# Seven products instead of eight for gate and up in FFN1's first half, with the sampled tokens moved into that half

## The chip, the cores and the metric

The kernel runs on one core of one Trainium2 chip. The metric is device time in microseconds (us) of one launch. A profiled execution gives, beside its time, a trace of every instruction: the engines are TensorE (PE; its weight loads are listed as PEld), VectorE (DVE), ScalarE (ACT), GpSimd (POOL), and SyncE (SP), which here issues nearly all DMAs.

## The reference

One inference step of one decoder layer in float32: 1024 prompt tokens in one sequence, and 32 sampled tokens (8 sequences of 4, with caches). Model width 1024, FFN width 2816.

```python
def swiglu_ffn(x, w_gate, w_up, w_down):
    return (jax.nn.silu(x @ w_gate) * (x @ w_up)) @ w_down

def decoder_layer(x, ...):
    x = x + 0.5 * swiglu_ffn(rms_norm(x, ffn1[0]), ffn1[1], ffn1[2], ffn1[3])
    y, ... = token_mixer(rms_norm(x, mix[0]), ...)
    x = x + y
    x = x + 0.5 * swiglu_ffn(rms_norm(x, ffn2[0]), ffn2[1], ffn2[2], ffn2[3])
```

`token_mixer` projects to 1792 columns, runs an RG-LRU (a causal convolution of 4, two gates, a linear recurrence) beside sliding-window attention (8 query heads on 2 key heads, window 128), normalises both, and projects back. The sampled tokens go through the same layer with their own states and caches.

## The kernel before

**Arithmetic.** Activations lie transposed: 128 rows of the feature dimension on the partitions, tokens in the columns, eight such tiles (KD = 8) for width 1024. Every float32 operand of a product is split into a rounded part `hi` and the remainder `lo`, and a product is three matmuls, hi·hi, hi·lo, lo·hi, into the same PSUM bank. Weights are split on the core: ACT writes `whi` (L423), DVE `wlo` (L425); activations likewise into `xh` and `xl`, the FFN's hidden values into `ha`.

**Halves and units.** Tokens are handled in two halves: half 0 (g = 0) is prompt tokens 0 to 511, half 1 is prompt tokens 512 to 1023 and the 32 sampled tokens, 544 columns (`TW`). A product for half 0 is one matmul of 512 columns (L445 to L447); for half 1 it is two of 272 (CB) in two neighbouring banks (L455, L456). Weights come in units of 128 x 1024 (512 KB): a gate or up unit gives one tile f of 128 of the 22 hidden tiles (NF), with 8 k steps; a down unit gives two output tiles from a group of four hidden tiles (the first group: four outputs from two). A tile is thus a gate and an up unit, `gu(f)`; down units follow some tiles later (`DOWN`).

**Stages.** FFN1 of half 0; FFN1 of half 1 with half 0's mixer merged into it; FFN2 of half 0 with half 1's mixer merged in; FFN2 of half 1. `merge` sets each mixer unit at a position counted in FFN units (`POS`: for half 0 the q units at 5, 5, 27, 28, the out units from 47 on). The first tile of FFN1's half 1 is put before the last four down units of half 0.

**Seven products.** In FFN2's half 1, from its fourth tile on (`plain=3`), `gu7` computes gate and up of a tile together. The pair is seen as a 2 x 2 block matrix (gate and up as rows, the two halves of the 1024 inputs as columns), the tokens as 2 x 2 blocks (two halves of inputs, two times 272 tokens), and a variant of Strassen's scheme needs seven block products, P1 to P7, each 4 k x 3 matmuls of 272 columns (L778), where the plain way needs eight. For that, `sums` forms four sums of weight blocks on DVE (L388), `split_pair` splits seven blocks (L401 on ACT, L403 on DVE) into one of six weight slots each, and the token factors (`x1a`, `T1`, `T2`, `x2b`, `T3`, `x2a`, `T4`) are computed once for the half by `prenorm_pairs`. A pair's raw blocks and sums lie in slots of the pool `big`, eight for a pair. `ev7` joins the products and applies silu.

**Order.** `Sched` sets the order of all instructions when the program is built. Each piece of work is a generator that asks for an engine with an estimated duration and the times of what it depends on; the earliest start goes first, then the smaller priority number. `main` (priority 5) puts TensorE's units in the order of `plan`. `MAINCAP` limits the PSUM banks (of eight) that the units hold to six. On the chip each engine then runs its own list in order and waits on semaphores.

**First half's normalisation.** In FFN1's half 0 (`mode == "late"`) the products start on x times the gain, and the reciprocal root mean square (`rslot`, from `rstd_of`) is multiplied in when the gate product is evicted (`evg`, L644) and again after silu. For other halves `prenorm` normalises before the products (L560 to L569). `evd` (L680) adds a down product to x. `mixed` (L1480 to L1490) normalises the mixer's results into `xh` and `xl` for the out units; L1299 writes attention's output.

Of the kernel before, what the change touches and what calls it, by code (L numbers as in the profile page):

```python
# [75 lines left out]
MODES = (None, "tanh", "tanh")  # L76
MAINCAP = 6
# [144 lines left out]
def layer(ctx: ExitStack, tc, t):  # L222
# [12 lines left out]
    xh = [const.tile([128, KD, TW[g]], F32R, name=f"xh{g}") for g in range(2)]  # L235
    xl = [const.tile([128, KD, TW[g]], F32R, name=f"xl{g}") for g in range(2)]
# [61 lines left out]
    def dP(g, passes=1):  # L298
        return TW[g] / 2400 * passes * 1.01 + 0.01
# [61 lines left out]
    pairs = set()  # L361
    sum_of = {}

    def loader():
        n = 2 * FIRST - 1
        while n + 1 < len(order):
            n += 1
            if n in pairs:
                tk = yield Req("Q", 1.0, tok["xt",], big.soon(8), when=big.has(8), lat=4.0)
                raw_of[n], sum_of[n] = ([big.get()[0] for _ in range(4)] for _ in range(2))  # L370
                for i, r in enumerate(raw_of[n]):
                    SP.dma_start(F(r, 0), t["w"][order[n + i // 2], :, i % 2 * 512:i % 2 * 512 + 512])
                done(("raw", n, 0), tk)
                sc.spawn(sums(n), 2)
                n += 1
                continue
            tk = yield Req("Q", 0.6, raws.soon(), when=raws.has(), lat=4.0)
            raw_of[n] = raws.get()[0]
            load_piece(n, 0)
            done(("raw", n, 0), tk)  # L380

    def sums(n):

        g1, g2, u1, u2 = (F(i, 0) for i in raw_of[n])
        a, b, c, d = (F(i, 0) for i in sum_of[n])
        for i, (o, x, y, op) in enumerate(((a, u1, u2, OP.add), (b, a, g1, OP.subtract), (c, g2, b, OP.subtract), (d, g1, u1, OP.subtract))):
            tk = yield Req("D", 0.6, tok["raw", n, 0])
            V.tensor_tensor(o, x, y, op)  # L388
            done(("sum", n, i), tk)

    def split_pair(n):
# [4 lines left out]
        for i, (src, dep) in enumerate(((g1, 0), (ss[0], 1), (ss[1], 1), (ss[2], 1), (ss[3], 1), (g2, 0), (u2, 0))):  # L396
# [8 lines left out]
        big.put(Tok(max(tk.t, tok["sum", n, 3].t)), *raw_of[n], *ss)  # L405
# [54 lines left out]
    def group(n, j, g, srcs, deps):  # L460
# [3 lines left out]
        for k0 in range(0, m, 2):  # L464
            ks = range(k0, min(k0 + 2, m))
            ds = [deps[k] for k in ks]
            if k0 == 0:
                tk = yield Req("P", dP(g, 3) * len(ks), wait(n, 0), banks.soon(1 + g), *ds,
                               when=lambda: banks.has(1 + g)() and main_out[0] + g < (8 if tok['plain', 3, 1].t else MAINCAP))
# [23 lines left out]
    def proj(n, g, deps):  # L493
        return (yield from group(n, 0, g, [(xh[g][:, k], xl[g][:, k]) for k in range(KD)], deps))
# [37 lines left out]
    def xap(m, g):  # L532
        return F(X[g][m], g)

    def xsplit(st, name, g):

        for m in range(KD):
            tk = yield Req("A", dA(g, True), tok["x", st, g, m])
            S.activation(xh[g][:, m], xap(m, g), AF.Copy, scale=col(name, m))  # L539
            tk = yield Req("D", dD(g), tk)  # L540
            V.scalar_tensor_tensor(xl[g][:, m], xap(m, g), col(name, m), f32(xh[g][:, m]), op0=OP.mult, op1=OP.subtract)  # L541
            done(("xs", st, g, m), tk)

    def rstd_of(st, g, out):
        yield Req("A", 0.0, tok["x", st, g, 0], Tok(11.0), big.soon(3), when=big.has(3))
        tmp = [big.get()[0] for _ in range(3)]
        tk = yield from mean_rsqrt([xap(m, g) for m in range(KD)], [[tok["x", st, g, m]] for m in range(KD)], g, D,
                            F(out, g), *(F(i, g) for i in tmp))
        big.put(tk, *tmp)
        done(("rstd", st, g), tk)  # L550

    def prenorm(st, name, g):

        yield Req("A", 0.0, tok["x", st, g, 0], big.soon(4), when=big.has(4))
        tmp = [big.get()[0] for _ in range(4)]
        out, acc, sq, sq2 = (F(i, g) for i in tmp)
        tk = yield from mean_rsqrt([xap(m, g) for m in range(KD)], [[tok["x", st, g, m]] for m in range(KD)], g, D, out, acc, sq, sq2)
        ps_ = (acc, sq)
        tk = yield Req("D", dD(g), tok["xfree", st, g])
        V.scalar_tensor_tensor(ps_[0], xap(0, g), col(name, 0), out, op0=OP.mult, op1=OP.mult)  # L560
        for m in range(KD):
            p = ps_[m % 2]
            tka = yield Req("A", dA(g), tk)
            S.activation(xh[g][:, m], p, AF.Copy)
            if m < KD - 1:
                tk = yield Req("D", dD(g))
                V.scalar_tensor_tensor(ps_[(m + 1) % 2], xap(m + 1, g), col(name, m + 1), out, op0=OP.mult, op1=OP.mult)
            tkd = yield Req("D", dD(g), tka)
            V.tensor_tensor(xl[g][:, m], p, f32(xh[g][:, m]), OP.subtract)  # L569
# [4 lines left out]
    def xt(i, k):  # L574
        if i == 3:
            return xh[1][:, k, CB:], xl[1][:, k, CB:]
        o = (4 * i + k) * CB
        return tuple(x[0].rearrange("p k n -> p (k n)")[:, o:o + CB] for x in (xh, xl))

    def xsums(ys, k, tk):  # L580
        (y1a, y1b), (y2a, y2b) = ((ys[m][:, :CB], ys[m][:, CB:]) for m in (k, k + 4))

        for o, x, y in ((y1a, y1b, y1a), (y1b, y2b, y1b), (y2b, y2b, y1a), (y2a, y2a, y2b)):
            tk = yield Req("D", 0.35, tk)
            V.tensor_tensor(o, x, y, OP.subtract)
        done(("xsum", k), tk)

    def prenorm_pairs(st, name, g):

        yield Req("A", 0.0, tok["x", st, g, 0])  # L590
        big.put(Tok(0.0), *range(NBIG - 3, NBIG))
# [3 lines left out]
        done(("xt",), Tok(0.0))  # L595
        tk = yield from mean_rsqrt([xap(m, g) for m in range(KD)], [[tok["x", st, g, m]] for m in range(KD)], g, D, out, *ys[:3])
        yield Req("D", 0.0, tk, tok["xfree", st, g])
        for m in range(KD + 1):
            if m < KD:
# [13 lines left out]
        dh = 0.07 + CB * 1.04e-3

        def small(src, i, k, tk):
            h, l = xt(i, k)
            tka = yield Req("A", 0.33, tk, tok["xfree", st + 1, 0])
            S.activation(h, src, AF.Copy)
            tk = yield Req("D", dh, tka)
            V.tensor_tensor(l, src, f32(h), OP.subtract)  # L620
            done(("xt", i, k), tk)
        for i in range(4):
            if i == 3:
                yield Req("A", 0.0, tok["plain", st, g])
            for k in range(4):
                (y1a, y1b), (y2a, y2b) = ((ys[m][:, :CB], ys[m][:, CB:]) for m in (k, k + 4))
                yield from small((y1a, y2b, y1b, y2a)[i], i, k, tok["xsum", k])
                if i > 1:
                    big.put(tok["xt", i, k], tmp[1 + k + 4 * (i == 3)])
# [4 lines left out]
    def ffn(st, g, st2, u0, mode, rslot=None, plain=NF):  # L634


        H, spart = {}, {}
        fac = 0.25 if mode == "tanh" else 0.5

        def evg(b, tk, f):  # L640
            if mode == "late":
                tk = yield Req("D", dD(g), tk, tok["rstd", st, g], pff.soon(), when=pff.has())
                s = spart[f] = pff.get()[0]
                V.tensor_tensor(S_(F(s, g), g), P_(b, g), S_(F(rslot, g), g), OP.mult)  # L644
                mrelease(b, tk, g)
                tk = yield Req("A", dA(g), tk, sets=(S_SET,))
                S.activation(F(s, g), F(s, g), AF.Silu)
                tk = yield Req("D", dD(g), tk)
                V.tensor_tensor(F(s, g), F(s, g), F(rslot, g), OP.mult)
            elif mode == "silu":  # L650
                tk = yield Req("A", dA(g), tk, pff.soon(), when=pff.has(), sets=(S_SET,))
                s = spart[f] = pff.get()[0]
                S.activation(S_(F(s, g), g), P_(b, g), AF.Silu)
                mrelease(b, tk, g)
            else:
                tk = yield Req("A", dA(g), tk, pff.soon(), when=pff.has(), sets=TANH)
                s = spart[f] = pff.get()[0]
                S.activation(S_(F(s, g), g), P_(b, g), AF.Tanh, scale=0.5)
                tk = yield Req("D", dD(g), tk)
                V.scalar_tensor_tensor(S_(F(s, g), g), S_(F(s, g), g), 1.0, P_(b, g), op0=OP.add, op1=OP.mult)  # L660
                mrelease(b, tk, g)
            done(("s", st, g, f), tk)

        def evu(b, tk, f):
            tk = yield Req("D", dD(g), tk, tok["s", st, g, f])
            s = spart.pop(f)
            V.tensor_tensor(S_(F(s, g), g), P_(b, g), S_(F(s, g), g), OP.mult)
            mrelease(b, tk, g)
# [8 lines left out]
        def evd(b, tk, m, old, new):  # L677
            tk = yield Req("D", dD(g), tk, tok[old])
            x = S_(xap(m, g), g)
            V.scalar_tensor_tensor(x, P_(b, g), fac, x, op0=OP.mult, op1=OP.add)  # L680
# [1076 lines left out]
```

## Time and profile before

| | |
|---|---|
| median of 3 runs | 1827.89 us (1827.76 to 1827.99) |
| the profiled execution | 1827.96 us, its span from first to last instruction 1825.9 us, granted TensorE clock 0.999 |
| matmuls | 11406; 3168 of 272 columns and 1584 of 512 in FFN1 alone |
| moved by DMA | 187.98 MB, mean 103 GB/s |
| launch of a DMA to landing, median | 3.3 us for a weight unit of 512 KB, 4.9 us for a 256 KB block of a pair |

A row of a list of groups gives the line of the kernel, the engine, the operation, output and inputs, the shape and the count, then the busy time and the mean duration of one in ns. Matmuls overlap in the pipeline: one of 512 columns is listed with 390 ns, and the next starts 227 ns after it. A row of stretches gives the borders in us, its length, and the busy us and count of instructions for each engine.

### The profile page before, as it was taken

How to read it: one execution, taken by the hardware profiler on the slowest of the kernel's cores; microseconds unless marked ns; L12 is line 12 of the kernel's file. 1: busy time of each engine (PE TensorE's matmuls, PEld its weight loads, DVE VectorE, ACT ScalarE, POOL GpSimd, SP SyncE). 2: the span in 40 equal slices, each digit the busy share in tenths (PEclk: the TensorE clock that was granted, in tenths of full speed). 3: DMA queues.
4: the chain of work that ended last, by engine and by line, in shares of the span. 5: the costliest groups of instructions: out<-in, count | busy, mean ns of one | idle time of the engine just before them, and what ended most of it. 6: DMA issues, size and time to landing. Idle time of an engine off the chain costs nothing.

```text
span 1825.9 us, 28092 instructions
## 1 busy us (share of the span) xinstructions
PE 1819.2 (100%) x11406; PEld 1665.0 (91%) x11406; DVE 1179.5 (65%) x1898; ACT 860.8 (47%) x1363; POOL 12.3 (1%) x39
## 2 busy tenths in 40 slices
PE   9999999999999999999999999999999999999999
PEld 7888888899999999989988988888889899999999
DVE  6774444476665677645666677776664767767764
ACT  6442322344755476423456566674542444445442
POOL 0000000000000000000000000000000000000000
PEclk9999999999999999999999999999999999999999
DMA  5423223243222222422242332223242433233131
GB/s 175 145 93 104 93 98 121 93 137 109 94 87 94 93 70 80 129 93 93 82 156 95 106 101 84 83 91 106 87 137 91 139 116 102 73 110 110 59 116 73
DMA packets 65728, 187.98 MB, mean 103 GB/s; under 512 B 7984, under 2 KB 10544, under 8 KB 65584
## 3 DMA queue, kind: packets, MB, share of 16 engines
q1 hardware_dynamic: 65456, 186.10, 30.6%
q8 instruction: 89, 1.46, 0.3%
q14 instruction: 39, 0.32, 0.1%
q10 hardware_dynamic: 144, 0.10, 0.0%
HBM read 174.58 MB, written 9.90 MB: 101 GB/s over the span
## 4 chain that ended last, share of the span: by engine, by line
PE 99%; DMA 0%; DVE 0%; SPq 0%; ACT 0%; issue 0%
PE ps L456 19%; PE ps L455 19%; PE ps L445 16%; PE ps L446 15%; PE ps L447 15%; PE ps L778 11%; PE ps L1274 1%; PE ps L1009 0%; PE ps L1237 0%; PE ps L1236 0%; PE ps L1293 0%; PE ps L1292 0%; PE ps L1125 0%; PE ps L337 0%; DMA fa<-x 0%; PE ps L1400 0%
## 5 line engine op out<-in xcount | busy, mean ns | idle before, releaser
L423 ACT ACTIVATE whi<-raw 128x1024 fp32r<-128x1024 f32 (+1 forms) x274 | 285.0, 1040 | 524.3 <-PE ps L446 205.1
L425 DVE TENSOR_TENSOR wlo<-raw,whi 128x1024 fp32r<-128x1024 f32 (+1 forms) x274 | 328.7, 1200 | 80.8 <-ACT whi L423 76.3
L445 PE MATMUL ps<-xh,whi 128*128 128x512 f32 x880 | 344.9, 392 | 0.6 <-ACT xh L539 0.6
L446 PE MATMUL ps<-xl,whi 128*128 128x512 f32 x880 | 342.9, 390 | 0.6 <-DVE xl L541 0.6
L447 PE MATMUL ps<-xh,wlo 128*128 128x512 f32 x880 | 342.9, 390 | 0.0
L680 DVE SCALAR_TENSOR_TENSOR fa<-ps,fa 128x512 f32<-128x512 f32 (+1 forms) x192 | 135.5, 707 | 137.5 <-PE ps L456 73.6
L447 PEld LDWEIGHTS ps<-xh,wlo 128*128 128x128 f32 x880 | 165.2, 188 | 35.0
L445 PEld LDWEIGHTS ps<-xh,whi 128*128 128x128 f32 x880 | 165.3, 188 | 33.7 <-ACT xh L539 1.2
L446 PEld LDWEIGHTS ps<-xl,whi 128*128 128x128 f32 x880 | 165.3, 188 | 33.4 <-DVE xl L541 1.2
L456 PE MATMUL ps<-ha,whi 128*128 128x272 f32 x704 | 191.4, 291 | 0.0
L455 PE MATMUL ps<-ha,whi 128*128 128x272 f32 x704 | 190.0, 286 | 0.0
L455 PE MATMUL ps<-xh,whi 128*128 128x272 f32 x576 | 166.7, 289 | 0.0
L455 PE MATMUL ps<-xl,whi 128*128 128x272 f32 x576 | 166.5, 289 | 0.0
L456 PE MATMUL ps<-xh,wlo 128*128 128x272 f32 x576 | 166.3, 289 | 0.0
L456 PE MATMUL ps<-xh,whi 128*128 128x272 f32 x576 | 166.0, 288 | 0.0
L455 PE MATMUL ps<-xh,wlo 128*128 128x272 f32 x576 | 165.9, 288 | 0.0
L456 PE MATMUL ps<-xl,whi 128*128 128x272 f32 x576 | 165.0, 286 | 0.0
L778 PE MATMUL ps<-xh,wlo 128*128 128x272 f32 x532 | 153.8, 289 | 0.0
L778 PE MATMUL ps<-xl,whi 128*128 128x272 f32 x532 | 153.6, 289 | 0.0
L778 PE MATMUL ps<-xh,whi 128*128 128x272 f32 x532 | 152.5, 287 | 0.0
L445 PE MATMUL ps<-ha,whi 128*128 128x512 f32 x352 | 137.3, 390 | 0.0
L447 PE MATMUL ps<-ha,wlo 128*128 128x512 f32 x352 | 137.1, 389 | 0.0
(261 smaller groups left out, 3524.2 us busy)
## 6 DMA issues: line engine op xcount, KB each, us to landing
raw<-w SPq DMA_DIRECT2D x266, 512.0 KB, 3.3
fa<-w SPq DMA_DIRECT2D x80, 256.0 KB, 4.9
fa<-x SPq DMA_DIRECT2D x8, 272.0 KB, 3.9
xs<-fa SPq DMA_DIRECT2D x8, 272.0 KB, 5.7
fa<-xs SPq DMA_DIRECT2D x8, 272.0 KB, 3.0
y<-fa SPq DMA_DIRECT2D x8, 272.0 KB, 2.0
fa<-x SPq DMA_DIRECT2D x8, 256.0 KB, 4.6
xs<-fa SPq DMA_DIRECT2D x8, 256.0 KB, 4.3
```

What stands on the lines that cost most here:

```text
L423: S.activation(hi, raw, AF.Copy)
L425: V.tensor_tensor(lo, raw, f32(hi), OP.subtract)
L445: PE.matmul(p, wh, ah, start=first, stop=False)
L446: PE.matmul(p, wh, al, start=False, stop=False)
L447: PE.matmul(p, wl, ah, start=False, stop=last)
L455: PE.matmul(ps[:, b, :CB], w, a[:, c0], start=s, stop=e)
L456: PE.matmul(ps[:, b + 1, :CB], w, a[:, c1], start=s, stop=e)
L680: V.scalar_tensor_tensor(x, P_(b, g), fac, x, op0=OP.mult, op1=OP.add)
L778: PE.matmul(ps[:, bs[b], :CB], x, y, start=not after and k == j == 0, stop=k == 3 and j == 2, skip_group_check=bool(after))
L1274: PE.transpose(ps[:, bk, j * 128:(j + 1) * 128], P[j // 2][:, j % 2, hf * 128:(hf + 1) * 128], ident)
```

## The change

FFN1's first stage takes the wide layout: half 0 is joined by the 32 sampled tokens there (544 columns; the host lays them out between the two prompt halves), and half 1 of FFN1 has 512. `wide(st, g)` tells which of the two widths a half has in a stage. After FFN1 the 32 columns are copied by GpSimd from half 0's x to half 1's, so that the mixers and FFN2 have the halves of before. From tile 7 on (`FIRST7`), half 0's gate and up take the seven products. The token factors, computed by `factors` while the plain tiles run, lie in half 1's `xh`/`xl` buffers, in the key buffer `kb`, in four rows of `rm`, and `T4` in half 0's own `xh`/`xl` after the last plain tile. Half 1's x is no longer in place from the start: its slots hold raw weights, the normalised tokens, and then the pool `early` for every other pair. `prenorm` reads x once through one slot for the mean square; `load_b` loads it again when the pool is whole.

```diff
+FIRST7 = 7
-    xh = [const.tile([128, KD, TW[g]], F32R, name=f"xh{g}") for g in range(2)]
+    xh_ = [const.tile([128, KD * W], F32R, name=f"xh{g}") for g in range(2)]
...
+    def wide(st, g):
+        return 1 - g if st == 1 else g
-    big, pff, ... = Pool(range(16, NBIG - 3)), ..., Pool(range(NRM)), Banks()
+    big, early, pff, ... = Pool(range(16, NBIG)), Pool([]), ..., Pool(range(2)), Banks()
     def dP(g, passes=1):
-        return TW[g] / 2400 * passes * 1.01 + 0.01
+        return (TW[g] / 2400 + 0.013 * (1 + g)) * passes
 def loader():
-                tk = yield Req("Q", 1.0, tok["xt",], big.soon(8), when=big.has(8), lat=4.0)
-                raw_of[n], sum_of[n] = ([big.get()[0] for _ in range(4)] for _ in range(2))
+                st, pool = pairs[n]
+                tk = yield Req("Q", 1.0, tok["xt", st], pool.soon(7), when=pool.has(7), lat=4.0)
+                raw_of[n], sum_of[n] = ([pool.get()[0] for _ in range(k)] for k in (4, 3))
 def split_pair(n):
-        big.put(Tok(max(tk.t, tok["sum", n, 3].t)), *raw_of[n], *ss)
+            if i >= 4:
+                pairs[n][1].put(tk, *((g1, u1, *ss), (g2,), (u2,))[i - 4])
 def group(n, j, g, srcs, deps):
-  ... main_out[0] + g < (8 if tok['plain', 3, 1].t else MAINCAP)
+  ... main_out[0] + g < (8 if tok['plain', 3, 1].t or tok['rstd', 1, 0].t and not tok['x', 2, 0, 0].t else MAINCAP)
 def prenorm(st, name, g):
+        if st == 1:
+            yield Req("Q", 0.0, tok["h", 1, 0, NF - 11], early.soon(1), big.soon(3), when=...)
+            tmp, stage = [big.get()[0] for _ in range(3)], early.get()[0]
+            for m in range(KD):
+                tk = yield Req("Q", 0.6, tk, lat=4.0)
+                SP.dma_start(F(stage, w), t["x"][:, m, TW[1]:])
+                ... square on ACT, add on DVE
+            yield Req("A", 0.0, tok["h", 1, 0, NF - 4])
+            ... column_sums, rsqrt, load of the silu set
-        tk = yield Req("D", dD(g), tok["xfree", st, g])
+        tk = yield Req("D", dD(w), tok["xfree", st, g], tok["x", st, g, KD - 1])
+    FX = {1: {"x1a": (1, 0), "T1": (1, 1), "T2": (1, 2), "x2b": (1, 3), "T3": "kb", "x2a": "rm", "T4": (0, 0)},
+          3: {"T1": (0, 0), "T2": (0, 1), "T3": (0, 2)}}
+    def factors_of(ys, k):
+        for m in (k, k + 4):
+            V.scalar_tensor_tensor(ys[m], xap(m, 0, 1), col("g1", m), F(rslot, 1), op0=OP.mult, op1=OP.mult)
+        ... seven fsplit (ACT copy, DVE subtract) and four subtractions of 272 columns
+        early.put(tok["fx", 1, "T3", k], X[1][k])
+        yield Req("A", 0.0, tok["plain", 1, 0])
+        yield from fsplit(1, "T4", k, x2a, tk)
+        early.put(tok["fx", 1, "T4", k], X[1][k + 4])
 def evg(b, tk, f):
             if mode == "late":
+                if f < 2:
+                    ... S.activation(S_(F(s, w), w), P_(b, w), AF.Copy), bank released,
+                    then V.tensor_tensor(F(s, w), F(s, w), F(rslot, w), OP.mult)
 def evd(b, tk, m, old, new):
+            if new[:3] == ("x", 2, 0):
+                tk = yield Req("G", 0.2, tk)
+                G.tensor_copy(xap(m, 1, 1)[:, HALF:], xap(m, 0, 1)[:, HALF:])
 def load_b():
+        yield Req("Q", 0.0, early.soon(8), when=lambda: early.n() == 8 and tok["last",].t is not None)
         for m in range(KD):
-            tk = yield Req("Q", 0.6, Tok(60.0 + 4 * m), tok["w", 2 * FIRST - 1, 1], lat=4.0)
-            SP.dma_start(xap(m, 1), t["x"][:, m, HALF:])
+            tk = yield Req("Q", 0.6, lat=4.0)
+            SP.dma_start(xap(m, 1, 0), t["x"][:, m, TW[1]:])
-    plan, nxt = ffn(1, 0, 2, 0, "late", rslot), ffn(1, 1, 2, 0, MODES[1])
-    plan[-4:-4] = nxt[:1]
-    plan += merge(nxt[1:], mixer(0))
+    plan = ffn(1, 0, 2, 0, "late", rslot, plain=FIRST7) + merge(ffn(1, 1, 2, 0, MODES[1]), mixer(0))
+    def hold():
+        yield Req("Q", 0.0, tok["xfree", 2, 0], when=big.has(3))
+        ... three slots of big set aside, rows 2 to 5 of rm to its pool, GpSimd zeroes half of kb
```

`POS` stays as it is. The first tile of half 1 no longer runs before half 0's last four down units; of these, the first two run abreast (all four outputs on the first two hidden tiles, then on the last two), as at the end of FFN2.

More of the change, by code (lines that the diff above doesn't have):

```diff
@@ L359, in load_piece @@
         SP.dma_start(raw_ap(n, i), t["w"][order[n], :, pieces_of(n)[i]])
-    pairs = set()
+    pairs = {}
     sum_of = {}
@@ L373, in loader @@
                 done(("raw", n, 0), tk)
+                if st == 1 and n + 2 not in pairs and pairs.get(n + 6, (0,))[0] != 1:
+                    done(("last",), tk)
                 sc.spawn(sums(n), 2)
@@ L468, in group @@
                 tk = yield Req("P", dP(g, 3) * len(ks), wait(n, 0), banks.soon(1 + g), *ds,
-                               when=lambda: banks.has(1 + g)() and main_out[0] + g < (8 if tok['plain', 3, 1].t else MAINCAP))
+                               when=lambda: banks.has(1 + g)() and main_out[0] + g < (8 if tok['plain', 3, 1].t or tok['rstd', 1, 0].t and not tok['x', 2, 0, 0].t else MAINCAP))
                 b = banks.get(1 + g)
@@ L491, in abreast, with proj @@
         return [res[i] for i in range(len(parts))]
-    def proj(n, g, deps):
-        return (yield from group(n, 0, g, [(xh[g][:, k], xl[g][:, k]) for k in range(KD)], deps))
+    def proj(n, g, deps, w=None):
+        w = g if w is None else w
+        return (yield from group(n, 0, w, [(xh[g][w][:, k], xl[g][w][:, k]) for k in range(KD)], deps))
     def mrelease(b, tk, g):
@@ L542, in xsplit @@
             done(("xs", st, g, m), tk)
     def rstd_of(st, g, out):
+        w = wide(st, g)
         yield Req("A", 0.0, tok["x", st, g, 0], Tok(11.0), big.soon(3), when=big.has(3))
         tmp = [big.get()[0] for _ in range(3)]
-        tk = yield from mean_rsqrt([xap(m, g) for m in range(KD)], [[tok["x", st, g, m]] for m in range(KD)], g, D,
-                            F(out, g), *(F(i, g) for i in tmp))
+        tk = yield from mean_rsqrt([xap(m, g, w) for m in range(KD)], [[tok["x", st, g, m]] for m in range(KD)], w, D,
+                            F(out, w), *(F(i, w) for i in tmp))
@@ L549, in rstd_of @@
         big.put(tk, *tmp)
         done(("rstd", st, g), tk)
+        yield Req("A", LOAD)
+        sc.set = S_SET
+        sc.load_set(S_SET)
     def prenorm(st, name, g):
[L554 to L557, printed above, removed]
+        w = wide(st, g)
@@ L565, in prenorm @@
             if m < KD - 1:
[L566 to L569, printed above, removed]
+                tk = yield Req("D", dD(w))
+                V.scalar_tensor_tensor(ps_[(m + 1) % 2], xap(m + 1, g, w), col(name, m + 1), out, op0=OP.mult, op1=OP.mult)
+            tkd = yield Req("D", dD(w), tka)
@@ new lines, in fsplit, with quarters, factors @@
+    def fsplit(st, name, k, src, *deps):
+        h, l, _ = fx(st, name, k)
+        tka = yield Req("A", 0.33, *deps)
+        S.activation(h, src, AF.Copy)
+        tk = yield Req("D", 0.07 + CB * 1.04e-3, tka)
+        V.tensor_tensor(l, src, f32(h), OP.subtract)
+        done(("fx", st, name, k), tk)
+    def quarters(ys, k):
+        (x1a, x1b), (x2a, x2b) = ((ys[m][:, :CB], ys[m][:, CB:]) for m in (k, k + 4))
+        return x1a, x1b, x2a, x2b
+    def factors():
+        tk = yield Req("D", 0.0, tok["rstd", 1, 0], tok["w", 2 * FIRST - 1, 1])
+        done(("xt", 1), tk)
+        ys = [F(i, 1) for i in X[1]]
+        for k in range(4):
+            sc.spawn(factors_of(ys, k), 1)
@@ L584, in xsums, with factors_b @@
+    def factors_b(st, ys, slots, k, tk):
+        x1a, x1b, x2a, x2b = quarters(ys, k)
+        for o, x, y in ((x1a, x1b, x1a), (x1b, x2b, x1b), (x2b, x2b, x1a), (x2a, x2a, x2b)):
             tk = yield Req("D", 0.35, tk)
             V.tensor_tensor(o, x, y, OP.subtract)
-        done(("xsum", k), tk)
+        yield Req("A", 0.0, tok["xfree", st + 1, 0])
+        yield from fsplit(st, "T1", k, x1a, tk)
+        yield from fsplit(st, "T2", k, x2b)
+        yield from fsplit(st, "T3", k, x1b)
+        big.put(tok["fx", st, "T3", k], slots[k])
+        yield Req("A", 0.0, tok["plain", st, 1])
+        yield from fsplit(st, "T4", k, x2a)
+        big.put(tok["fx", st, "T4", k], slots[k + 4])
@@ L610, in prenorm_pairs @@
             if m >= 4:
-                sc.spawn(xsums(ys, m - 4, tkd), 3)
+                sc.spawn(factors_b(st, ys, tmp[1:], m - 4, tkd), 3)
         big.put(tkd, tmp[0])
[L613 to L629, printed above, removed]
     def xfree(st, g):
@@ L637, in ffn @@
         H, spart = {}, {}
+        w = wide(st, g)
         fac = 0.25 if mode == "tanh" else 0.5
@@ L701, in gu @@
                 xfree(st2, g)
+                if st == 1 and not g:
+                    xfree(1, 1)
             if f == plain - 1:
@@ L786, in gu7 @@
                 xfree(st2, g)
+                if st == 1 and not g:
+                    xfree(1, 1)
         xv = {m: ("x", st, g, m) for m in range(KD)}
@@ L802, in down @@
             if gi == len(GROUPS) - 1 and m0 == 0:
-                for j, (b, tk) in enumerate((yield from abreast([group(ns[j // mp], j % mp, g, srcs, deps) for j in range(nu * mp)]))):
+                for j, (b, tk) in enumerate((yield from abreast([group(ns[j // mp], j % mp, w, srcs, deps) for j in range(nu * mp)]))):
                     end(j, b, tk)
@@ L807, in down @@
                 for j in range(mp):
-                    b, tk = yield from group(ns[0], j, g, srcs, deps)
+                    b, tk = yield from group(ns[0], j, w, srcs, deps)
                     end(j, b, tk)
@@ L823, in ffn @@
         for f in range(NF):
-            steps.append((lambda f=f: gu(f) if f < plain else gu7(f), 2, f >= plain))
+            steps.append((lambda f=f: gu(f) if f < plain else gu7(f), 2, f >= plain and (st, early if st == 1 and f > plain and f % 2 == NF % 2 else big)))
             if f in DOWN:
@@ L1585, in layer @@
         if getattr(fn, "seven", False):
-            pairs.add(len(order))
+            pairs[len(order)] = fn.seven
         order += us
@@ L1594, in free_rslot @@
     def free_rslot():
-        yield Req("D", 0.0, tok["s", 1, 0, NF - 1])
-        big.put(tok["s", 1, 0, NF - 1], rslot)
+        yield Req("D", 0.0, tok["s", 1, 0, FIRST7 - 1], *(tok["y", k] for k in range(4)))
+        big.put(tok["s", 1, 0, FIRST7 - 1], rslot)
     def finish(g):
@@ L1609, in cached @@
         SP.dma_start(t["osv"], t["cv"][:, NT:])
-    tok["xfree", 1, 1].t = 0.0
+    held = []
+    def hold():
+        yield Req("Q", 0.0, tok["xfree", 2, 0], when=big.has(3))
+        held.extend(big.get()[0] for _ in range(3))
+        rms.put(tok["xfree", 2, 0], *range(2, NRM))
+        tk = yield Req("G", 4.0, tok["xfree", 2, 0])
+        for v in range(2):
+            G.memset(f32(kb[64 - 64 * v:128 - 64 * v, 2 + v]), 0.0)
+        done(("kb0",), tk)
     sc.spawn(loader(), 0)
@@ L1625, in layer @@
     sc.spawn(free_rslot(), 2)
+    sc.spawn(hold(), 0)
+    sc.spawn(factors(), 2)
     sc.spawn(cached(), 4)
```

235 lines of the change are left out of this document (146 added, 89 removed).

## The prediction

> **What bounds the kernel now.** I read the engine totals, the clock and the chain first, then TensorE's waits, and only then single stretches.
>
> ```profile
> PE 1819.2 (100%) x11406; PEld 1665.0 (91%) x11406; DVE 1179.5 (65%) x1898; ACT 860.8 (47%) x1363; POOL 12.3 (1%) x39
> ...
> PEclk9999999999999999999999999999999999999999
> ...
> PE 99%; DMA 0%; DVE 0%; SPq 0%; ACT 0%; issue 0%
> ...
> PE ps L866 <- DVE rm L864: 1.6, 1, 1.6
> PE ps L445 <- ACT xh L539: 0.6, 1, 0.6
> PE ps L446 <- DVE xl L541: 0.6, 2, 0.3
> ```
>
> The chain that sets the end is 99% TensorE, at full clock, and these three waits, 2.8 us, are all that TensorE has. A busy TensorE could still be slow, so the cadence decides: stretches cut at the borders of a group give the time of one matmul in the stream.
>
> ```profile
> core 0: us, PE busy (x) PEld busy (x) DVE busy (x) ACT busy (x) POOL busy (x), PEclk, DMA share, GB/s
> 855.60:891.69 36.09, 36.09 (x291) 36.09 (x289) 24.18 (x31) 15.07 (x21) 0.00 (x0) 1.00 0.26 89
> ...
> 1632.98:1675.13 42.15, 42.15 (x338) 42.15 (x337) 30.91 (x51) 24.60 (x48) 0.00 (x0) 1.00 0.19 65
> 1675.13:1699.44 24.31, 24.31 (x195) 24.31 (x194) 16.80 (x26) 6.07 (x10) 0.00 (x0) 1.00 0.43 149
> 313.20:345.84 32.64, 32.64 (x145) 27.04 (x144) 14.52 (x17) 8.95 (x11) 0.00 (x0) 1.00 0.33 112
> 291.44:313.20 21.76, 21.76 (x97) 18.02 (x96) 11.01 (x13) 4.79 (x6) 0.00 (x0) 1.00 0.36 120
> ```
>
> In this order: three plain gate/up tiles of a 544-token half (12.03 us each; a matmul or two in each count hangs over from the neighbours), four seven-product tiles of such a half (10.54), four of its down units (6.08 each), three plain tiles of a 512-token half (10.88), four of its down units (5.44). A 272-column matmul costs 125.4 ns (42.15/336), a 512-column one 226.7 (32.64/144). The kernel is a sum of matmuls: fewer of them is less time, unless something then makes TensorE wait.
>
> **The change, part by part.**
>
> Products. A plain tile of 544 tokens is 2 units x 8 k x 3 passes x 2 = 96 matmuls, a seven-product tile 7 x 4 x 3 = 84. Fifteen tiles (f = 7 to 21) change: 15 x (12.03 - 10.54) = 22.4 us; by counts, 180 x 125.4 ns = 22.6. I take 22.4.
>
> Beside the rows, the Trainium skill ("TensorE: Matmul & The Clock Gate", Back-to-back issue gap) gives a warm matmul N/2.4 + 2.5 ns: an estimate of 115.8 ns for 272 columns, and 180 of them would save 20.8 us. The rows differ, 125.4 ns, and decide.
>
> Sampled tokens. The first half becomes 544 wide, the second 512. FFN1 keeps one half of each width, so 22 tiles and 22 down units of each kind change places: 0 in matmuls. Not so in cover: the second half's FFN1, under which the first half's mixer runs, gets shorter by 22 x (12.03 - 10.88) + 22 x (6.08 - 5.44) = 39 us. This is the part to fear.
>
> Work for the seven products. Each pair of units needs four DVE sums (0.68) and seven splits on ACT (0.62) and DVE (0.68) in place of two long ones. FFN2 does that already: in the second row above DVE is busy 30.91 of 42.15 us, ACT 24.60, and TensorE never waits, nor at the step from the last such tile to the down units:
>
> ```profile
> L388 DVE TENSOR_TENSOR fa<-fa x76: 680/684/694, 1467.9 to 1783.7; 128x512 f32<-128x512 f32 x76
> ...
> L401 ACT ACTIVATE whi<-fa x131: 614/623/637, 1482.6 to 1792.0; 128x512 fp32r<-128x512 f32 x131
> ...
> L403 DVE TENSOR_TENSOR wlo<-fa,whi x133: 680/684/694, 1476.7 to 1792.6; 128x512 fp32r<-128x512 f32 x133
> ...
> 1797.38 0.29 PE L778 MATMUL ps<-xh,wlo 128*128 128x272 f32 x1
> 1797.50 0.29 PE L455 MATMUL ps<-ha,whi 128*128 128x272 f32 x1
> ```
>
> The token factors are new in FFN1: 8 scalings, 16 differences and 28 splits of 272 columns, at
>
> ```profile
> L601 DVE SCALAR_TENSOR_TENSOR fa<-fa,cols x8: 776/778/785, 1434.3 to 1454.7; 128x544 f32<-128x544 f32 x8
> ...
> 1577.64 0.43 DVE L726 TENSOR_TENSOR fa<-fa 128x272 f32<-128x272 f32 x1
> ...
> 1568.22 0.40 ACT L707 ACTIVATE fa<-ps 128x272 f32<-128x272 f32 x1 [1.12 <-PE ps L778]
> ...
> 62.00:358.00 296.00, 296.00 (x1352) 247.30 (x1351) 158.60 (x219) 91.71 (x115) 0.00 (x0) 1.00 0.33 111
> ```
>
> so DVE 8 x 0.78 + 44 x 0.43 = 25 us and ACT 28 x 0.40 = 11 us, all but T4 under seven plain tiles and eight down units, 7 x 12.0 + 8 x 6.1 = 133 us, in a half where DVE is idle 46% of the time (last row): 0. T4's four splits have the four down units after tile 6, 24 us: 0.
>
> Weights of the pairs and the second half's x come over SP's queue:
>
> ```profile
> fa<-w SPq DMA_DIRECT2D x80, 256.0 KB, 4.9
> ...
> fa<-x SPq DMA_DIRECT2D x8, 256.0 KB, 4.6
> ```
>
> Two pools of seven slots take turns: one pair loads while the other is split. A load of 4.9, sums 2.7 and seven splits 7 x 1.3 = 9 make 17 us, against two tiles, 21 us: hidden, 0. With one pool it would not be (a rival).
>
> The second half's x is loaded twice (eight pieces for the mean square, eight for use, 2 MB more), queued behind the pairs, at 4.6 us a piece and a DMA share of 0.2 to 0.4: hidden by the tiles before. Its scaling waits for the end of tile 21, whose factors lie in those buffers: 16 x 0.7 = 11 us of DVE inside the last four down units. These have DVE busy 16.80 of 24.31 us: 28 asked of 24.3. But a tile's last k is needed 4 us after its first, and splits of later units can slip. I take 0; ends 0 and 4.
>
> Start. Each x piece grows by 16 KB while a tile's pace slows from 10.88 to 12.03; against the 1.2 us of waits on xh and xl above I take +0.3 (ends -0.5 and +1.5). A group now takes two banks, so eight fill sooner. What frees them is the mean square:
>
> ```profile
> 34.18 0.69 DVE L510 SCALAR_TENSOR_TENSOR fa<-ps,fa 128x512 f32<-128x512 f32 x1 [2.11 <-ACT fa L508]
> ...
> 37.43 0.68 DVE L644 TENSOR_TENSOR fa<-ps,fa 128x512 f32<-128x512 f32 x1
> ```
>
> Evictions with it begin at 37.4; tile 2's up product, which fills the eighth bank, ends near 6.2 + 3 x 12.0 = 42, and the first two gates leave earlier by an ACT copy: 0.
>
> Later stages. FFN2's second half keeps its 19 seven-product tiles, with seven slots a pair for eight: 0. The 32 columns that GpSimd copies, and its zeroing of the key buffer, lie on an engine that is 1% busy; the first use of either is tens of us later: 0.
>
> **Where time comes back: the mixer's end.** The out projection needs all of attention. The rows: the start of q's last unit (605.35) and of the first out unit (775.25), attention's last output, the last normalised operand, and DVE's load between.
>
> ```profile
> 605.35 0.40 PE L445 MATMUL ps<-xh,whi 128*128 128x512 f32 x1
> ...
> 775.25 0.40 PE L445 MATMUL ps<-xh,whi 128*128 128x512 f32 x1
> ...
> 779.35 0.39 PE L445 MATMUL ps<-xh,whi 128*128 128x512 f32 x1
> ...
> L1299 DVE TENSOR_TENSOR fa<-ps,fa x8: 676/686/696, 653.6 to 737.2; 64x512 f32<-64x512 f32 x8
> ...
> L1490 DVE TENSOR_TENSOR xl<-fa,xh x8: 681/683/686, 733.0 to 772.2; 128x512 fp32r<-128x512 f32 x8
> ...
> 605.00:773.00 168.00, 168.00 (x1228) 161.63 (x1227) 126.06 (x264) 100.81 (x201) 0.56 (x1) 1.00 0.28 91
> ```
>
> From q to the last operand: 772.9 - 605.35 = 167.5 us; the operand is used in the seventh or eighth k, at 779.35 or later: 6.5 us to spare. The order puts 19 FFN units between (positions 28 to 47), now 512 wide: 19 x (6.05 - 5.44) = 11.6 us less cover. If the mixer's own work took as long as before, TensorE would wait 11.6 - 6.5 = 5 us. DVE is 75% and ACT 60% busy there, so the chain is not one full engine but many short steps; some sixty FFN evictions become 0.03 us shorter, 2 us, and TensorE's slots between FFN groups come sooner. I take 3 us; ends 0 and 15 (the list order of attention's eight blocks may change either way).
>
> The mixer's beginning is nearer than it was but holds:
>
> ```profile
> 379.86 0.69 DVE L680 SCALAR_TENSOR_TENSOR fa<-ps,fa 128x512 f32<-128x512 f32 x1 [0.58 <-PE ps L447]
> ...
> L569 DVE TENSOR_TENSOR xl<-fa,xh x8: 682/686/693, 397.5 to 409.9; 128x512 fp32r<-128x512 f32 x8
> ...
> 416.21 0.40 PE L445 MATMUL ps<-xh,whi 128*128 128x512 f32 x1
> ```
>
> 30.7 us from the last down eviction to the last operand, against three tiles of 10.88 = 32.6 us: 0.
>
> The sum: 1827.96 (the profiled execution; span 1825.9; the runs' median is 1827.89) - 22.4 + 0.3 + 3 = 1808.9.
>
> **The rivals.**
> 1. Nothing comes back. The spare 6.5 us and the shorter evictions hold the mixer up: 1827.96 - 22.4 = 1805.5. For it: no wait anywhere in the present trace.
> 2. The mixer is late by 10 to 15 us, because blocks of attention meet in another order, or because q and k of the first half meet the late scaling: 1818. Against: 5 us is what the rows give.
> 3. The clock. Ten 512-column matmuls at the very start take 4.00 us,
>
> ```profile
> 1.64 4.00 PE L866 MATMUL ps<-rm 128*128 128x512 f32 x10 [1.64 <-DVE rm L864]
> ```
>
> 0.40 each against 0.227 later: half speed, some 1.7 us lost. A wait of 5 us at the out projection could bring that back: 1827.96 - 22.4 + 0.3 + 5 + 1.7 = 1812.6. The Trainium skill ("TensorE: Matmul & The Clock Gate", Part 1) says that an idle window of about 3.4 us puts the clock to half. No wait of this trace after the start is long enough to show it, and the forecast's own wait is 3 us, so its chance is small.
> 4. Slower: the pairs starve. If the two pools don't alternate in effect (the mean square's staging holds one slot, the scaled sums three), a pair takes its 17 us in a row while its tile takes 10.54: 6 us lost a tile, 15 x 6.2 = 93, 1827.96 - 22.4 + 93 = 1898. It decides from 1.49 us of wait a tile. Against: FFN2 shows the same work with no wait.
>
> **How the numbers follow.** Forecast, 1.5 to 7 us given back: 0.5, 1808.9, own range 1807 to 1812.5. Rival 1: 0.25. Rival 2: 0.13. Rival 3: 0.05. Rival 4: 0.07, of which little stays within 0.2% (3.7 us, about what a measurement of this kernel can tell from no change). The range 1804 to 1818 leaves out rival 4 and half of rival 2. Faster 0.91, same 0.03, slower 0.06.
>
> **What would show it.** 180 fewer matmuls in all; L778's counterpart with 3 x 952 in place of 3 x 532 matmuls; tiles 7 to 21 of the first half at 10.5 us; TensorE waits only at the start and, some us, before the first out unit of the first half's mixer, on the DVE that writes its operand. Wrong would be waits before the seven-product matmuls on splits or sums (rival 4), at the second half's first tile, or a 272-column cadence above 126 ns.

## The result and the profile after

The changed kernel takes 1813.97 us (median of 4 runs, 1813.64 to 1814.26) against 1827.94 of the kernel before beside it: a ratio of 0.9922, interval 0.9905 to 0.9939. The profiled execution has a span of 1812.5 us, 13.4 less than before. The page of the changed kernel, totals, clock, chain and the costliest groups of the seven products:

```profile
PE 1802.1 (99%) x11226; PEld 1643.3 (91%) x11226; DVE 1257.1 (69%) x2087; ACT 932.7 (51%) x1542; POOL 15.4 (1%) x47
...
PEclk9999999999999999999999999999999999999999
...
PE 98%; DVE 1%; DMA 0%; issue 0%; ACT 0%; SPq 0%; DVEq 0%
...
L890 PE MATMUL ps<-xh,wlo 128*128 128x272 f32 x832 | 240.6, 289 | 0.0
```

There are 180 matmuls fewer, at full clock; DVE has 78 us more work. L890 is the seven-product line: 832 matmuls of each kind read `xh` or `xl`, and 120 more in FFN1's fifteen tiles (15 x 2 products x 4 k) read factors that lie in the key buffer and in `rm`: 952, as forecast. TensorE's waits follow: whom it waited for, us in total, times, the longest:

```profile
PE ps L980 <- DVE rm L978: 1.6, 1, 1.6
PE ps L460 <- DVE fa L786: 0.9, 2, 0.6
PE ps L470 <- DVE fa L786: 0.8, 1, 0.8
PE ps L1351 <- DVE fa L786: 0.6, 2, 0.3
PE ps L461 <- DVE xl L616: 0.6, 2, 0.4
PE ps L470 <- ACT xh L558: 0.5, 1, 0.5
PE ps L1124 <- DVE fa L772: 0.4, 1, 0.4
PE ps L1389 <- DVE fa L786: 0.4, 1, 0.4
PE ps L470 <- DVE xl L560: 0.3, 1, 0.3
PE ps L461 <- DVE ha L778: 0.3, 1, 0.3
```

Three groups of waits have become ten. Four of them, 2.7 us together, are on down evictions (L786), after which a PSUM bank is free again. The list adds up to 6.4 us against 2.8, but it tells too little: it counts from the modelled end of a matmul, and neighbouring matmuls overlap:

```profile
422.82 0.39 PE L462 MATMUL ps<-xh,wlo 128*128 128x512 f32 x1
423.05 0.39 PE L460 MATMUL ps<-xh,whi 128*128 128x512 f32 x1
423.59 0.50 PE L461 MATMUL ps<-xl,whi 128*128 128x512 f32 x1 [0.16 <-DVE xl L616]
```

The third starts 0.54 us after the second, not 0.227: 0.31 us are lost where the list says 0.16. So I count from start to start, stage by stage, from the first matmul of a stage to the first of the next. The rows that bound the third stage (FFN2 of half 0 with the second mixer), before and after:

```profile
916.00 0.40 PE L445 MATMUL ps<-xh,whi 128*128 128x512 f32 x1
...
1451.73 0.28 PE L455 MATMUL ps<-xh,whi 128*128 128x272 f32 x1
...
899.61 0.39 PE L460 MATMUL ps<-xh,whi 128*128 128x512 f32 x1
...
1438.52 0.28 PE L470 MATMUL ps<-xh,whi 128*128 128x272 f32 x1
```

| us | stage 1: FFN1, half 0 | stage 2: FFN1, half 1, first mixer | stage 3 | stage 4: FFN2, half 1 |
|---|---|---|---|---|
| before | 373.44, with half 1's first tile | 536.35, without it | 535.73 | 374.17 |
| before, by the matmuls of after | 378.4 | 509.0 | 535.7 | 374.2 |
| after | 380.44 | 513.10 | 538.91 | 373.95 |
| given back | 2.0 | 4.1 | 3.2 | -0.2 |

The second row is the first with one 12.03 us tile moved, and with the forecast's prices for what each stage gained and lost (in stage 1, 7 plain tiles wider by 1.15 us, 15 tiles shorter by 0.34 and 22 down units wider by 0.64). Of the 22.4 us that the products were to save, 9 came back in three stages: most of it as short waits of TensorE, and 0.8 us of stage 1 as a slower cadence, told below.

### The profile page after: what moved, and what is told of

It is laid out like the page before. It is cut to its first block, busy times and chain, and to the rows that moved or that the text cites. A ratio compares the mean times of both kernels' runs of the same rounds, so it can differ in the third digit from the quotient of the medians.

```text
span 1812.5 us, 28292 instructions
## 1 busy us (share of the span) xinstructions
PE 1802.1 (99%) x11226; PEld 1643.3 (91%) x11226; DVE 1257.1 (69%) x2087; ACT 932.7 (51%) x1542; POOL 15.4 (1%) x47
## 4 chain that ended last, share of the span: by engine, by line
PE 98%; DVE 1%; DMA 0%; issue 0%; ACT 0%; SPq 0%; DVEq 0%
PE ps L890 20%; PE ps L460 15%; PE ps L461 15%; PE ps L462 15%; PE ps L471 14%; PE ps L470 14%; PE ps L1389 1%; PE ps L1351 0%; PE ps L1124 0%; PE ps L1352 0%; PE ps L1407 0%; PE ps L1408 0%; PE ps L1240 0%; PE ps L348 0%; DMA fa<-x 0%; DVE fa L786 0%
## 5 line engine op out<-in xcount | busy, mean ns | idle before, releaser
L890 PE MATMUL ps<-xh,wlo 128*128 128x272 f32 x832 | 240.6, 289 | 0.0
L890 PE MATMUL ps<-xl,whi 128*128 128x272 f32 x832 | 239.9, 288 | 0.0
L890 PE MATMUL ps<-xh,whi 128*128 128x272 f32 x832 | 239.4, 288 | 0.0
L415 ACT ACTIVATE whi<-fa 128x512 fp32r<-128x512 f32 x238 | 147.6, 627 | 123.3 <-PE ps L471 103.9
L786 DVE SCALAR_TENSOR_TENSOR fa<-ps,fa 128x544 f32<-128x544 f32 (+1 forms) x192 | 135.0, 706 | 97.9 <-PE ps L471 60.1
L462 PEld LDWEIGHTS ps<-xh,wlo 128*128 128x128 f32 x880 | 165.2, 188 | 34.8
L461 PEld LDWEIGHTS ps<-xl,whi 128*128 128x128 f32 x880 | 165.3, 188 | 34.7 <-DVE xl L616 1.7
L460 PEld LDWEIGHTS ps<-xh,whi 128*128 128x128 f32 x880 | 165.3, 188 | 33.5 <-DVE fa L772 0.5
L417 DVE TENSOR_TENSOR wlo<-fa,whi 128x512 fp32r<-128x512 f32 x238 | 159.4, 687 | 49.3 <-ACT whi L415 48.5
L890 PEld LDWEIGHTS ps<-xh,whi 128*128 128x128 f32 x832 | 156.8, 188 | 0.0
L890 PEld LDWEIGHTS ps<-xl,whi 128*128 128x128 f32 x832 | 156.5, 188 | 0.0
L890 PEld LDWEIGHTS ps<-xh,wlo 128*128 128x128 f32 x832 | 156.5, 188 | 0.0
L460 PE MATMUL ps<-ha,whi 128*128 128x512 f32 x352 | 138.4, 393 | 0.9 <-DVE fa L786 0.9
L461 PE MATMUL ps<-ha,whi 128*128 128x512 f32 x352 | 137.2, 390 | 0.3 <-DVE ha L778 0.3
```

What stands on the lines that cost most here:

```text
L415: S.activation(hi, F(src, 0), AF.Copy)
L417: V.tensor_tensor(lo, F(src, 0), f32(hi), OP.subtract)
L460: PE.matmul(p, wh, ah, start=first, stop=False)
L461: PE.matmul(p, wh, al, start=False, stop=False)
L462: PE.matmul(p, wl, ah, start=False, stop=last)
L786: V.scalar_tensor_tensor(x, P_(b, w), fac, x, op0=OP.mult, op1=OP.add)
```

## Experiments

All ratios are to the kernel before on the same chip. Stage lengths come from each run's trace, read as above.

**The cost formula, undone.** The order of all instructions is made from cost estimates when the program is built. The change also rewrote TensorE's: 1.394 to 1.516 us for two k of a 544-token group, which takes 1.50; 1.313 to 1.358 for 512 tokens, which takes 1.36.

```diff
 def dP(g, passes=1):
-    return (TW[g] / 2400 + 0.013 * (1 + g)) * passes
+    return TW[g] / 2400 * passes * 1.01 + 0.01
 def gu7(f):
-    dur = 12 * (CB / 2400 + 0.0125)
+    dur = 12 * CB / 2400 * 1.01
```

> The changed kernel, but the builder's list order is made with the TensorE cost formulas of the kernel before (they take a 272-column group 7% and a 512-column group 4% too short). Theory A (the waits come from the cost formula: exact TensorE costs leave no slack in the order, so TensorE meets DVE evictions that are a little late): the waits after the first 50 us fall from 8 us to about 3, time about 1809 us. Theory B (the waits come from the change's own extra DVE work and the thinner cover): they stay, 1812 to 1816 us.

Measured: 1819.3 us, ratio 0.9954 (0.9941 to 0.9968), slower than the changed kernel. But stage 3 took 535.62 us, that of before to 0.1, while stages 1 and 2 took 382.21 and 518.62, 1.8 and 5.5 more than with the exact formula. Theory A is right for stage 3 and wrong for the others: the old formula is worse there. Stage 2 now waits where the forecast had put its wait, in the first out unit, on the mixer's last operands (L1605, second row). The first row is a wait of stage 1, after the first group of down units; the changed kernel waits there too, but for less:

```profile
PE ps L470 <- DVE fa L786: 2.9, 1, 2.9
PE ps L461 <- DVE xl L1605: 1.7, 3, 1.1
```

**The cost formula alone, in the kernel before** (the same lines, the other way).

> The kernel before, its list order made with the changed kernel's TensorE cost formulas, nothing else. Theory A: waits of 3 to 5 us appear, 1831 to 1833 us. Theory B: no change, 1827 to 1829 us.

Measured: 1831.01 us, ratio 1.0018 (1.0009 to 1.0026), as theory A has it. Stages 1, 2 and 4 are those of before within 0.1; stage 3 takes 538.81 us, 3.1 more, with the waits that the changed kernel has there:

```profile
PE ps L445 <- DVE fa L680: 0.6, 1, 0.6
PE ps L1274 <- DVE fa L680: 0.4, 1, 0.4
PE ps L1236 <- DVE fa L680: 0.3, 1, 0.3
PE ps L446 <- DVE ha L673: 0.3, 1, 0.3
```

(L680 is L786 after, L1274 is L1389, L1236 is L1351, L673 is L778: four waits for four, of the same lengths in the third stage.) So the 3.2 us of stage 3 come from the formula, not from FFN1.

**Fewer tiles.** `FIRST7 = 13` in place of 7.

> The changed kernel with the seven products from tile 13 on (9 tiles in place of 15). If a tile's worth is 1.49 us and what came back is fixed (layout, order): 1814.0 + 6 x 1.49 = 1822.9 us. If what came back grows with the number of seven-product tiles: 1827.9 - 9/15 x 14.0 = 1819.5 us.

Measured: 1829.7 us, ratio 1.0008 (0.9999 to 1.0017), worse than both expectations. The trace accounts for it: the span is 1827.9 us, 15.4 more than after. Six tiles at 1.49 are 8.9, and 6.5 us are new: 1.2 net in stage 1 (390.59 for 380.44, less the 8.94), where the first seven-product matmuls wait on a split (first row; why that split is late was not taken apart), and 4.9 in stage 3 (543.83 us for 538.91), where nothing was edited (second and third row). Some 1.6 of these 4.9 are the clock: behind the wait of 2.1 us it is granted at 0.50 from 1126.67 to 1130.08 us, and eight matmuls of 512 columns take 3.4 us in place of 1.8.

```profile
PE ps L890 <- DVE wlo L417: 2.0, 2, 1.5
...
PE ps L460 <- DVE mxt L1357: 2.1, 1, 2.1
PE ps L1408 <- DVE rm L1399: 1.1, 1, 1.1
```

The price of a tile agrees with this account. That the waits are fixed, or that they grow with the tiles, does not: they come out anew with each order.

**More latency in the plan**, of the changed kernel and of the kernel before.

```diff
-    def __init__(self, eng, dur, *deps, sets=None, when=None, lat=0.15, bias=0.0):
+    def __init__(self, eng, dur, *deps, sets=None, when=None, lat=0.4, bias=0.0):
```

> The changed kernel; the builder's list order assumes 0.40 us in place of 0.15 from the end of an instruction to the start of one that waits for it on another engine. Theory A (waits come from an order without slack): 2 to 4 us less, 1810 to 1812 us. Theory B: 1812 to 1816 us, no better.

> The kernel before, with its list order made under the assumption of 0.40 us in place of 0.15 between engines, the edit that cost the changed kernel 12.7 us. Theory C (an order is a draw: any new one brings some waits, with or without the change to FFN1): 5 to 12 us of waits here too, 1833 to 1840 us. Theory B (the change's thinner cover and denser DVE work make the order fragile): at most 3 us, 1828 to 1831 us.

Measured: 1826.63 us, ratio 0.9993 (0.9985 to 1.0002), for the changed kernel, 12.7 more than without the edit; 1842.03, ratio 1.0077 (1.0062 to 1.0091), for the kernel before, 14.3 more. Theory A's cure makes it worse, and theory B falls too: the kernel before is no less fragile, and its time lies above even theory C's 1833 to 1840 us. In the changed kernel stages 2 and 3 take 520.11 and 542.45. Among the waits are 2.5 us in the first out unit, before its fifth k step, again at the place that the forecast feared. Behind them the clock is at half (PEclk is the column before the DMA share):

```profile
PE ps L460 <- ACT xh L1600: 2.5, 1, 2.5
...
766.66:770.08 3.42, 3.41 (x9) 2.06 (x8) 2.69 (x5) 1.26 (x2) 0.00 (x0) 0.50 0.64 166
770.08:773.49 3.41, 3.41 (x16) 2.76 (x15) 1.92 (x2) 1.60 (x2) 0.00 (x0) 1.00 0.40 141
```

This is the prediction's third rival at the very place where it was put, though in another order. From 768.04 on the matmuls run 0.43 us apart in place of 0.227; as the last operands are written until 769.5, how much of the time lost there is the clock's alone is open. In the kernel before with the longer latency, stage 3 takes 546.02 against 535.73, and there too the clock is at half for 3.4 us. Beside these two, the orders of before and after are favourable ones: one changed estimate costs about as much as the whole change brings (14.0 us).

**Old formula from stage 3 on.**

```diff
 def dP(g, passes=1):
+    if tok["x", 2, 1, 0].t is not None:
+        return TW[g] / 2400 * passes * 1.01 + 0.01
     return (TW[g] / 2400 + 0.013 * (1 + g)) * passes
```

(and `gu7`'s old duration in FFN2.)

> The changed kernel with its exact TensorE cost formulas up to the end of FFN1, and the old, too short ones from there on. The third stage (first half's FFN2 with the second half's mixer) waited 5.6 us with the exact formulas and 2.5 us with the old ones, in both layouts. Theory (these 3 us come from the cost formula and not from the change to FFN1): waits before that stage stay as in the changed kernel, 3 us go, 1811 us. Rival (each new list order draws its waits anew): waits elsewhere change too, 1812 to 1818 us.

Measured: 1814.8 us, ratio 0.9927 (0.9915 to 0.994). In the profiled execution, the slowest of five, stage 2 took 513.16, as in the changed kernel. The four waits of stage 3 went, but new ones came around the sampled tokens' attention, and stage 3 took 541.28. The third rival is at work here as well, two waits and then the clock:

```profile
1214.18 0.50 PE L462 MATMUL ps<-rm 128*128 128x512 f32 x1 [1.75 <-DVE fa L1416]
...
1215.93 0.39 PE L462 MATMUL ps<-kb,rm 128*128 128x32 f32 x1 [0.51 <-DVE m L1476]
...
1210.00:1214.20 4.20, 2.45 (x12) 1.69 (x10) 1.96 (x3) 3.06 (x4) 0.00 (x0) 1.00 0.00 1
1214.20:1218.00 3.80, 3.29 (x12) 2.67 (x13) 3.48 (x10) 1.63 (x4) 0.00 (x0) 0.67 0.83 280
1218.00:1222.00 4.00, 4.00 (x11) 3.11 (x10) 3.49 (x8) 1.56 (x3) 0.00 (x0) 0.50 0.00 1
```

After 2.3 us of waits some twelve 512-column matmuls run 0.43 us apart in place of 0.227: 2.4 us more. The runs of this kernel lie between 1812.82 and 1816.62, with mean clocks from 1.000 to 0.998.

**The factors' scalings first.** In the changed kernel TensorE loses 1.0 us after the first group of down units (68.39 to 69.52, less the 0.125 of a matmul): DVE runs two scalings (L669, which read x) ahead of the down evictions (L786, which overwrite x).

```profile
66.91 1.48 DVE L669 SCALAR_TENSOR_TENSOR fa<-fa,cols 128x544 f32<-128x544 f32 x2
68.30 0.44 DVE L646 TENSOR_TENSOR xl<-fa,xh 128x272 fp32r<-128x272 f32 x1
68.65 1.35 DVE L786 SCALAR_TENSOR_TENSOR fa<-ps,fa 128x544 f32<-128x544 f32 x2
...
68.39 0.28 PE L471 MATMUL ps<-ha,wlo 128*128 128x272 f32 x1
69.52 0.36 PE L470 MATMUL ps<-xh,whi 128*128 128x272 f32 x1 [0.85 <-DVE fa L786]
```

```diff
 def factors():
-    for k in range(4):
-        sc.spawn(factors_of(ys, k), 1)
+    for m in (0, 4, 1, 5, 2, 6, 3, 7):
+        tk = yield Req("D", dD(1))
+        V.scalar_tensor_tensor(ys[m], xap(m, 0, 1), col("g1", m), F(rslot, 1), op0=OP.mult, op1=OP.mult)
+        if m > 3:
+            done(("y", m - 4), tk)
+            sc.spawn(factors_of(ys, m - 4), 1)
```

(`factors_of` starts with the differences; `factors` is spawned with priority 1.)

> The changed kernel with the eight scalings that make the factors' source issued first, ahead of all splits and differences. Down evictions overwrite x only after these scalings; TensorE waited 1.1 us for such an eviction after the first group of down units. Theory: that wait goes, 1813 us, if the rest of the order holds. Rival (order drawn anew): 1812 to 1820 us.

Measured: 1812.59 us, ratio 0.9917 (0.9904 to 0.9931), 1.4 less than the changed kernel. The wait is gone, and stages 2 to 4 stay within 0.1, so its cause is shown. Stage 1 takes 378.44 us, 2.0 less, and not all of that is this wait: about half lies at the first group of down units, and half at the start, where the first tile does not wait on x's splits in this execution (0.5 and 0.3 us in the list of the changed kernel). The edit does not touch that start.

**The first q units later.** `POS[0]["q"]` from (5, 5, 27, 28) to (7, 7, 27, 28).

> The changed kernel with the first half's first two q units one tile later (positions 7, 7 in place of 5, 5). They waited 0.9 us on the normalised operand, and a chain of small waits follows up to 460 us. Theory (the three tiles before them got shorter than the normalisation): the 0.9 us go, 1812.5 to 1813.5 us. Rival (order drawn anew): 1814 to 1820 us.

Measured: 1821.96 us, ratio 0.9968 (0.9956 to 0.9981). The edit missed its aim: x's first unit, at position 6, took q's place and waited 0.9 us on the same operand. Stage 3 drew 545.64 us, with the clock at 0.50 for 3.4 us of it. So the edit was made once more, on top of the scalings first, with x's first two units at 8 as well:

```diff
-POS = ({"k": 19, "v": 21, "q": (5, 5, 27, 28), "x": (6, 8, 12, 24), ...
+POS = ({"k": 19, "v": 21, "q": (7, 7, 27, 28), "x": (8, 8, 12, 24), ...
```

> The version with the scalings first (1812.6 us), and the first three mixer units of the first half (both q at 7, x at 8) after four tiles in place of three, so that no mixer unit takes q's place. Theory (three tiles of 10.9 us are too short a cover for the normalisation of the first half): the 0.9 us of waits for the normalised operand go, 1811.7 us. Rival (order drawn anew): they go, but others come, 1812 to 1822 us.

Measured: 1817.93 us, ratio 0.9949 (0.9936 to 0.9962). The waits for the normalised operand are gone and stage 2 is 1.0 us shorter (512.08 for 513.08), but stage 3, whose order was still made with the exact formula, takes 545.12 us.

**Together.** The scalings first and the old formula from stage 3 on; then the later mixer units with them.

> The version with the scalings first and the old TensorE cost formulas from the third stage on. If the 3 us of waits of that stage can be had back and no other wait is drawn: 1809.5 us. If the single long wait of the mixed formulas (6.3 us before the sampled tokens' attention) comes again: 1814 us.

> Scalings first, old cost formulas from the third stage on (1809.1 us), and the first three mixer units one tile later. The later units took away 1.8 us of waits between 400 and 450 us but drew 8 us of new ones in the third stage, whose order had the exact formulas. If the old formulas keep the third stage at its 2.5 us whatever comes before: 1807.3 us. If any new order of the second stage redraws the third all the same: 1810 to 1816 us.

Measured: 1809.12 us, ratio 0.9898 (0.9884 to 0.9912), stage 3 at 535.48; then 1808.39, ratio 0.9894 (0.9878 to 0.9911), stages of 378.30, 512.05, 535.58 and 374.05. The second is shorter than the changed kernel by 2.1 us in stage 1 (1.0 of it at the start), 1.0 in stage 2 and 3.3 in stage 3, and it beats both kernels, though it misses its own 1807.3 by 1.1 us. The long wait of the mixed formulas did not come again.

## Why the prediction was right and where its steps failed

The time lies in the stated range, faster as forecast; the point, 1808.9, was 5 us short. The forecast gave back 3.3 us and the chip 9, and not where it was forecast. That is more than the 1.5 to 7 us of the forecast's own band (1807 to 1812.5 us): the time is inside 1804 to 1818 because that range was wide, not because the waits were foreseen.

**Products: right.** There are 180 matmuls fewer, and 1.49 us a tile also fits the run from tile 13. A four-tile stretch in FFN1 is 0.2 us longer than one in FFN2 (42.15 us, before and after):

```profile
263.31:305.68 42.37, 42.37 (x339) 42.37 (x337) 31.27 (x52) 25.07 (x48) 0.00 (x0) 1.00 0.31 105
```

That is 126.1 ns a matmul for 125.4, or 0.8 us over the fifteen tiles, and just past the 126 ns that the prediction had named as a sign of being wrong. It is so for all seven products, whichever buffer they read; no run here tells why. The rival of the starving pairs had no part: in the changed kernel there is no wait at all before these tiles. (Its price was also added up a little low: 17 less 10.54 is 6.5 us a tile, 97 in all.)

**The mixer's end: the step that failed.** The forecast took 11.6 us of cover away from a chain of fixed length and waited 3 us. The cover went: from the last q unit's small matmuls to the first out unit there are 160.4 us before (614.9, first row, to 775.25) and 149.8 after (607.3 to 757.09, second and last row). But the chain is shorter too:

```profile
L1125 PE MATMUL ps<-bd,fa x8: 165/251/251, 614.9 to 615.6; 128*128 128x2 f32 x8
...
L1240 PE MATMUL ps<-bd,fa x8: 165/251/251, 607.3 to 608.0; 128*128 128x2 f32 x8
...
L1414 DVE TENSOR_TENSOR fa<-ps,fa x8: 674/688/695, 640.9 to 717.9; 64x512 f32<-64x512 f32 x8
...
L1605 DVE TENSOR_TENSOR xl<-fa,xh x8: 683/684/689, 722.1 to 754.6; 128x512 fp32r<-128x512 f32 x8
...
757.09 0.39 PE L460 MATMUL ps<-xh,whi 128*128 128x512 f32 x1
```

The last operand is there 148 us after those matmuls, 158 before, and the first out unit does not wait. The operand is used in its eighth k step, at 761.85, so that 6.6 us are to spare, about as much as before. The chain has no length of its own: no engine is full there (DVE 75% before), and its many short steps take the places that the list gives them. The kernel before shows it in three orders of the same work: 158.0 us as it was, 140.7 with the cost formula alone (613.7 to 754.4), 165.3 with the longer latency (619.5 to 784.8). So the mistake was to take the old length, less 2 us, for the new one. That the first out unit does not wait is the doing of this list and was not foreseen: with other estimates in the builder, two orders of the changed kernel waited just there, 1.7 and 2.5 us.

**The mixer's beginning: mis-sized at 0.** Its chain was taken as 30.7 us, the duration before. After the late scaling of half 1's x it took 39.0, from the last down eviction (386.7) to the last operand:

```profile
L616 DVE TENSOR_TENSOR xl<-fa,xh x8: 682/685/692, 407.5 to 425.0; 128x512 fp32r<-128x512 f32 x8
```

The cover was 32.6 us. TensorE lost 0.9 us to this, and 1.0 of stage 2 was recovered when the mixer began a tile later. Here the chain did lengthen, and the trace has the new work in front of it on DVE: in the 6.7 us up to that eviction DVE is busy for 6.4, and the last sum for the mean square starts 8.2 us after it (394.9), where before it started 2.0 us after it (381.9). The 0 for the scaling itself was right: half 1's first tile waits for nothing. The second rival had named the late scaling among its reasons for 10 to 15 us; here it cost 0.9.

**Token factors: mis-sized at 0.** They fit DVE's idle time, as forecast, but the forecast summed work and did not ask what is queued behind it: down evictions that overwrite x. This cost 1.0 us, shown by the scalings put first.

**Start: right.** The forecast was 0.3 us. From start to start the first tile loses 1.3 us for 1.1 before.

**Later stages: the other failed 0.** The cost formula is in the diff and had no term. It cost 3.2 us in stage 3, shown from three sides: in the kernel before with the formula alone, and in the changed one with the old formula throughout (535.62 us) or, beside the scalings first, from stage 3 on (535.48).

What remains of stage 2's 4.1 us is open: about 3 us between 450 and 830 us, in losses of 0.6 us or less, of which the list of waits names evictions for a part. No experiment took it apart. The clock's rival stands as a mechanism in other orders (2.4 us after 2.3 us of waits, 1.6 after 2.1), but no wait of the changed kernel set it off: its clock is 1.000.

## What to carry to other kernels

When one engine is full and its order is fixed in advance, a change's price has two parts: the work it takes off, which the cadence gave here to 0.8 us in 22, and the waits of the new order, which it does not give at all. Here four edits of an estimate alone made the kernel 3 to 14 us slower; a fifth, the old formula from stage 3 on, cost 0.8 us by itself and gave 3.5 back beside the scalings first. Count waits from start to start, stage by stage, and compare stages that the edit did not touch: they tell what is the order's doing. A diff's cost estimates and priorities are part of the change, and want a run of their own, in the old kernel too.

## What the runs showed of the hardware

In the traces of five of the orders tried, the granted TensorE clock fell to half in the middle of the kernel. With the mixed formulas it did so after waits of 1.75 and 0.51 us with a few small matmuls between them, for 6.8 us (1215.51 to 1222.33). From tile 13, and with the longer latency in the changed kernel, it did so after one wait of 2.1 and one of 2.5 us, for 3.4 us each. It did not after a single listed wait of 2.9 us with the old formula (3.1 us from start to start more than usual; the matmuls behind it 125 ns apart again). So the length of a wait does not decide alone.

The steps of the clock suggest why. Within a trace they lie whole multiples of 3.413 us apart: with the longer latency the clock rises at 5.49 us, falls at 766.66, which is 223 of them later, and rises again at 770.08. On that grid the wait of 2.1 us and 2.2 of the 2.5 us fall between two borders, while the 2.9 us (67.96 to 70.90) are parted by the border at 69.36 into 1.4 and 1.5. How much idle time between two borders is too much, these runs do not tell: 1.5 us dropped the clock with the q units later and did not with the old formula.

The Trainium skill ("TensorE: Matmul & The Clock Gate", Part 1) speaks of an idle window of about 3.4 us, free-running. The length agrees with the 3.413 us here; but the waits above are shorter than that, so the windows need not be wholly idle. That the runs of the kernel with the mixed formulas differed by up to 3.8 us agrees with a window that does not start with the kernel.
